# A second scaled stream for the queries, and key copies by transfer, in a two-layer decoder trunk

## The chip, the cores and the metric

One core of one Trainium2 chip runs the whole program. The metric is the time of one execution in microseconds (us) on the device; lower is better.

## What is computed

Two layers over 512 tokens of width 1024, all in float32. Layer 0 is a gated linear recurrence (HGRN2) with a gated ConvFFN behind it. Then keys and values are projected once from the normed stream. Layer 1 is differential attention with those keys and values, with a ConvFFN behind it, and a last norm. The part that matters here, cut from the reference:

```python
def rmsnorm(x, g):
    y = x32 * lax.rsqrt(jnp.mean(x32 * x32, axis=-1, keepdims=True) + EPS)
    return (y * g.astype(jnp.float32)).astype(x.dtype)

def shared_kv(x, kv_norm, kv_w):
    kv = rmsnorm(x, kv_norm) @ kv_w
    k = kv[..., :DA_QDIM].reshape(B, T, DA_HEADS, 2, DA_HEAD_DIM)
    v = kv[..., DA_QDIM:].reshape(B, T, DA_HEADS, DA_V_DIM)
...
    h = rmsnorm(x, norm_mix[li])
    q = (h @ w_q).reshape(B, T, DA_HEADS, 2, DA_HEAD_DIM) * (DA_HEAD_DIM ** -0.5)
    s = jnp.einsum('bqhcd,bkhcd->bhcqk', qb, k) + bias
    p = jax.nn.softmax(s, axis=-1)
    attn = p[:, :, 0] - lam * p[:, :, 1]
    o = jnp.einsum('bhqk,bkhv->bqhv', attn, v)
```

Keys and values read the stream scaled by `kv_norm`, queries the same stream scaled by `norm_mix[1]`; the factor of the norm, one per token, is common to both. A vector over the 1024 features can be multiplied either into the stream or into the rows of the weight.

## The kernel before

The stream lies transposed in SBUF as eight tiles `x0` to `x7` of 128 features by 512 tokens. A float32 product is made of three products of the fp32r type: each operand is split into a high part (a cast on ACT) and the rest (a subtraction on DVE), and `mm3` (lines 104 to 106) issues high by high, high by low and low by high. `split` does both halves of a split; with a gain it multiplies it in (lines 62 and 63, ACT and DVE), without one it casts and subtracts (lines 59 and 60). `x_split(n, g)` splits tile `n` into `xh`, `xl`. `on_tile`, from `stage` in `build`, is called as each tile of the new stream is done: it splits the tile, squares it on ACT and adds the square to `acc` on DVE.

Weights are streamed. `stage` (line 81) issues a load of 128 x 1024 floats on SP's queue into one of three buffers `wst`, and, if a gain is given, multiplies it in on POOL (line 86). Then `whi` is cast on ACT (line 59, or 775 in the attention) and `wlo` made on DVE (line 60, or 778), each in one of three buffers.

The attention stage, `attention`, is where the change lies. The stream reaches it unscaled (`stage("plain")`), and all 24 loads of key, query and value weights carry a gain, index 2 for keys and values and 3 for queries. The order of the work on PE, DVE, ACT and POOL is the order in which the code issues it; SP's order is left to the scheduler. There are two sequences, woven together:

- `products()` is a generator of projections, in units. A unit is one step of the sum for a key or query projection (three products of 512 columns), or two steps for a block of the values (six of 256 columns). Eight units are one projection of a head's keys, or queries, or two blocks of a pair's values. `units(n, most)` advances it by `n`, and lets `some(most)` issue up to `most` waiting steps of splitting keys and queries (`side`) and three of the small chain of a head's output norm (`chain`, lines 1047 and 160 to 166). When a projection is done, `evac` scales it by the norm's factor into `kq` (DVE, line 848); `keys` then casts each half of it into `kh` on ACT (line 869), writes a copy of the half into the other 64 partitions on POOL (line 870), and subtracts into `kl` on DVE (line 876); `queries` does likewise into `qs` (856, 859).
- The loop over `b` goes through 32 blocks of 128 queries, four a head. A block's way is: `scores` (PE, lines 980 and 981, then a masked minimum with the bias `nb` on DVE, 983), `powers` (exponentials on ACT, 989), `weigh` (the two softmaxes joined into `at`, DVE, 1004), `turn` (PE transposes `at`, 1011, ACT copies it, 1013), `gather` (PE, 1024). In one pass, `scores` is issued for block `b + 2`, `weigh` for `b + 1`, `turn` and `gather` for `b`, with 2 + 3 + 1 units of projections between them (`U1`, `U2`, `U3`).

The opening of the stage: head 0's keys and queries are projected without their last step, with the sums of `acc` (line 183) and the norm's factor (`rms`, `rows`: lines 193 to 203, the factor is `rcol_n`) between them; then come the last steps, `U0` = 8 units, and the loop. `minus_lambda` makes the scalar `lam` from a tiny product, an exponential `lme` on ACT (line 748) and two steps on DVE. `bias(h0)` fetches the bias of two heads.

Of the kernel before, what the change touches and what calls it, by code (L numbers as in the profile page):

```python
# [19 lines left out]
P = 128  # L20
T = 512
# [8 lines left out]
U0, U1, U2, U3 = 8, 2, 3, 1  # L30
PIECES = {0: 1, 1: 3, 3: 6, 6: 8}
WARM = 8

# [3 lines left out]
class Trunk:  # L37
# [34 lines left out]
        self.split(self.x[n], hi, lo, g)  # L72
        return hi, lo

    def stage(self, src, width=1024, gain=None, k0=0, cols=P):

        st = self.wp.tile([P, 1024], F32, tag="wst", name="wst", bufs=3)
        dst = st[:, :width]
        if len(src.shape) == 3:
            dst = dst.rearrange("p (n k) -> p n k", n=src.shape[1])  # L80
        self.nc.sync.dma_start(dst, src)
        if gain is not None:
            n = width // cols
            w = st[:, :width].rearrange("p (k c) -> p k c", k=n)
            g = self.gains[:, gain, k0:k0 + n].unsqueeze(2).broadcast_to([P, n, cols])
            self.nc.gpsimd.tensor_tensor(w, w, g, ALU.mult)  # L86
        return st

    def weight_tiles(self):
# [643 lines left out]
    def attention(self, xkv, acc, on_tile):  # L733
# [3 lines left out]
        with ExitStack() as ctx:  # L737
# [16 lines left out]

            nbs = {}

            def bias(h0):

                nb = nbs[h0 // 2] = ap.tile([P, 2, T], F32, tag="nb", name="nb")
                nc.gpsimd.memset(nb[:, :, 0:256], 0.0)  # L760
                rows = self.bdram[h0:h0 + 2]
                nc.sync.dma_start(nb[:, :, 256:T], bass.AP(rows.tensor, rows.offset + P - 1,
                                                           [[382, P], [P * 383, 2], [1, 256]]))


            class Load:
                def __init__(me, src, gain=None, k0=0, cols=P):
                    me.src, me.gain, me.k0, me.cols = src, gain, k0, cols

                def stage(me):  # L770
                    me.st = self.stage(me.src, 1024, me.gain, me.k0, me.cols)

                def high(me):
                    me.w = self.weight_tiles()
# [10 lines left out]
            K = [[Load(a["w_kq"][2 * h], 2)] for h in range(NH)]  # L785
            Q = [[Load(a["w_kq"][2 * h + 1], 3)] for h in range(NH)]
            V = [[Load(a["w_v"][p, hf], 2, 4 * hf, 256) for hf in range(2)] for p in range(NH // 2)]
# [56 lines left out]
            qs, ks, vs = {}, {}, {}  # L844

            def evac(ps, scale=1.0):
                t = ap.tile([P, T], F32, tag="kq", name="kq")
                v.scalar_tensor_tensor(t, ps, scale, rb, ALU.mult, ALU.mult)
                return t

# [10 lines left out]
            def keys(h, ps):  # L861

                k = evac(ps)
                hi = ap.tile([P, 2, T], F32R, tag="kh", name="kh")
                lo = kls[h % 2]
                ks[h] = hi, lo

                def high(c, own, other):
                    s.copy(hi[own, c], k[own])
                    nc.gpsimd.tensor_copy(hi[other, c], k[own])  # L870

                for c, (own, other) in enumerate(parts):
                    side.append(lambda c=c, own=own, other=other: high(c, own, other))
                for c, (own, other) in enumerate(parts):
                    side.append(lambda c=c, own=own:
                                v.tensor_tensor(lo[own, c], k[own], hi[own, c].bitcast(F32), ALU.subtract))  # L876


            def product(load, done):
                ps, (hi, lo) = self.bank(), take(load)  # L880
                for k in range(KD):
                    c = slice(k * P, (k + 1) * P)
                    self.mm3(ps, (hi[:, c], lo[:, c]), xkv[k], k == 0, k == KD - 1)
# [51 lines left out]
            def pair(p):  # L935
                yield from product(K[2 * p][0], lambda ps: keys(2 * p, ps))
                yield from product(Q[2 * p][0], lambda ps: queries(2 * p, ps))
                yield from product(K[2 * p + 1][0], lambda ps: keys(2 * p + 1, ps))
                yield from product(Q[2 * p + 1][0], lambda ps: queries(2 * p + 1, ps))
                yield from values(p, range(4))  # L940

            def products():
                yield from product(K[1][0], lambda ps: keys(1, ps))
                yield from values(0, (0, 1))
                yield from product(Q[1][0], lambda ps: queries(1, ps))
                yield from values(0, (2, 3))
                for p in range(1, NH // 2):
                    yield from pair(p)
# [19 lines left out]
            def scores(b):  # L968
                h, i = divmod(b, 4)
                if i == 0:  # L970
                    heads[h] = [self.sp.tile([P, 2, 4], F32, tag="sums", name="sums"),
                                self.sp.tile([P, 4], F32, tag="r0", name="r0"),
                                self.sp.tile([P, 4], F32, tag="oms", name="oms")]
                n = (i + 1) * P
                oi = slice(i * P, n)
                sc = [self.bank("sc")[:, :n] for c in range(2)]
                st = self.sp.tile([P, 2], F32, tag="stat", name="stat", bufs=4)
                pt = ap.tile([P, 2, T], F32, tag="p", name="p")
                for c in range(2):
                    mm(sc[c], qs[h][:, c, oi], ks[h][0][:, c, 0:n], start=True, stop=False)  # L980
                    mm(sc[c], qs[h][:, c, oi], ks[h][1][:, c, 0:n], start=False, stop=True)  # L981
                for c in range(2):
                    v.tensor_tensor_reduce(sc[c], sc[c], nbs[h // 2][:, h % 2, T - n:], 1.0, 3e38, ALU.add, ALU.min,  # L983
                                           st[:, c:c + 1])
# [44 lines left out]
            def close(h):  # L1029

                sums, r0, ms, po = heads.pop(h)
                o = ap.tile([P, T], F32, tag="o", name="o")
# [19 lines left out]
                return turn_back  # L1052

            with tc.manual_schedule(engines=ORDERED):
                first = [(self.bank("sc"), take(w[0])) for w in (K[0], Q[0])]
                steps, got = self.norm_steps(acc, "n1", "sc")
                self.proj_first(first, xkv, KD - 1, steps)
                live.clear()
                rb, rc = got[1]
                keys(0, first[0][0])  # L1060
                queries(0, first[1][0])
                some(8)
                units(2)
                split_next()
                units(2)
                split_next()
                units(U0 - 4)
# [58 lines left out]
def build(tc, a, o, stop=None):  # L1126
    nc = tc.nc
    with ExitStack() as ctx:
# [1 line left out]
        t.enter(ctx)  # L1130
        t.setup()

        def stage(g):
            acc = t.sp.tile([P, T], F32, tag="acc", name="acc")
            xs = []

            due = []

            def on_tile(n):
                for add in due:  # L1140
                    add()
                due.clear()
                if g is not None:
                    xs.append(t.x_split(n, None if g == "plain" else g))
# [123 lines left out]
```

## Time and profile before

| | us |
|---|---|
| median of 3 runs (lowest, highest) | 1261.74 (1260.07, 1262.15) |
| the profiled execution | 1260.14 |
| its span, first to last instruction | 1258.4 |
| POOL busy in the span | 76.1 |
| granted PE clock, mean | 0.995 |

The profile is one execution. Engines are PE (matrix products), PEld (its weight loads), DVE (vector), ACT (scalar), POOL (GpSimd) and SP (here only issuing transfers). A row of a timeline is start, duration, engine, line, operation, outputs, inputs, shapes and count, and in brackets the time that the engine stood idle ahead of it and what ended that. A row of groups has the busy time, the mean of one in ns, and the idle time ahead, by what ended it. The attention stage runs from about 635 to 862 us. Matmuls are pipelined: a product of 512 columns is shown as 0.39 us though the next starts 0.23 us later, so times between starts are what counts.

### The profile page before, as it was taken

The page shows a single profiled execution, that of the slowest core. Times are in us where ns is not written, and L with a number is a line of the kernel's source. Part 1 is how long each engine was busy: PE and PEld are TensorE (multiplying, and loading weights), DVE is VectorE, ACT ScalarE, POOL GpSimd, SP SyncE. Part 2 cuts the span into 40 slices and gives each one's busy share as a digit, 9 for nine tenths or more (in the row PEclk, how much of TensorE's full clock was granted, in tenths as well). Part 3 has the DMA queues.
Part 4 walks back from the last instruction along what each step waited for, and adds up shares of the span by engine and source line. Part 5 has one row for each costly group of instructions (what it writes and reads, how often), then busy time and mean ns, then how long its engine had stood idle before and what let it go on. Part 6 is the DMA issues. An engine that isn't in the chain of part 4 may idle for free.

```text
span 1258.4 us, 18026 instructions
## 1 busy us (share of the span) xinstructions
PE 1232.3 (98%) x6994; PEld 1042.5 (83%) x6994; DVE 869.6 (69%) x1651; ACT 570.4 (45%) x993; POOL 76.1 (6%) x68
## 2 busy tenths in 40 slices
PE   9999999999999999999999989999999999999997
PEld 8888898888888888888888879798888888888886
DVE  6988979587777777533467988877787777762223
ACT  6555555454444444322245556655454444442221
POOL 0000000000000000000134422200000000000001
PEclk9999999999999999999999899999999999999998
DMA  6223222133323333333232211212233333232322
GB/s 229 69 84 120 85 85 65 54 118 100 92 93 101 101 99 89 100 94 92 97 101 71 73 51 59 85 68 84 84 101 100 101 100 89 96 92 92 104 80 68
DMA packets 38269, 115.36 MB, mean 92 GB/s; under 512 B 3960, under 2 KB 9896, under 8 KB 38184
## 3 DMA queue, kind: packets, MB, share of 16 engines
q1 hardware_dynamic: 37144, 113.27, 28.4%
q8 instruction: 55, 0.90, 0.3%
q10 hardware_dynamic: 1040, 0.94, 0.2%
q14 instruction: 30, 0.25, 0.1%
HBM read 112.09 MB, written 3.68 MB: 92 GB/s over the span
## 4 chain that ended last, share of the span: by engine, by line
PE 85%; DVE 10%; ACT 3%; issue 2%; DMA 0%; POOL 0%; SPq 0%; POOLq 0%; ACTq 0%; DVEq 0%
PE mm L105 25%; PE mm L106 25%; PE mm L104 25%; DVE wlo L60 1%; DVE wlo L778 1%; PE po L1024 1%; PE sc L104 1%; PE sc L105 1%; PE sc L106 1%; PE tp L1011 1%; DVE kl L876 1%; DVE sd L473 1%; ACT whi L59 1%; DVE sc L983 1%; PE sc L981 1%
## 5 line engine op out<-in xcount | busy, mean ns | idle before, releaser
L104 PE MATMUL mm<-xh,whi 128*128 128x512 f32 x1008 | 398.4, 395 | 0.1
L105 PE MATMUL mm<-xl,whi 128*128 128x512 f32 x1008 | 394.2, 391 | 0.5 <-DVE xl L63 0.5
L106 PE MATMUL mm<-xh,wlo 128*128 128x512 f32 x1008 | 393.7, 391 | 0.0
L60 DVE TENSOR_TENSOR wlo<-wst,whi 128x1024 fp32r<-128x1024 f32 (+1 forms) x172 | 208.1, 1213 | 145.7 <-ACT whi L59 143.7
L59 ACT CAST whi<-wst 128x1024 fp32r<-128x1024 f32 (+1 forms) x172 | 177.2, 1034 | 240.9 <-PE mm L105 185.3
L106 PEld LDWEIGHTS mm<-xh,wlo 128*128 128x128 f32 x1008 | 189.7, 188 | 39.6 <-DVE wlo L778 0.2
L105 PEld LDWEIGHTS mm<-xl,whi 128*128 128x128 f32 x1008 | 190.0, 189 | 39.2 <-DVE xl L63 2.0
L104 PEld LDWEIGHTS mm<-xh,whi 128*128 128x128 f32 x1008 | 190.1, 189 | 38.8 <-ACT whi L59 0.7
L104 PE MATMUL mm<-hh,whi 128*128 128x512 f32 (+1 forms) x374 | 141.0, 377 | 0.0
L105 PE MATMUL mm<-hl,whi 128*128 128x512 f32 (+1 forms) x374 | 140.8, 377 | 0.0
L106 PE MATMUL mm<-hh,wlo 128*128 128x512 f32 (+1 forms) x374 | 140.8, 376 | 0.0
L684 DVE TENSOR_TENSOR u<-mm,rbc_f 128x512 f32<-128x512 f32 x88 | 60.2, 688 | 73.4 <-PE mm L106 73.4
L104 PEld LDWEIGHTS mm<-hh,whi 128*128 128x128 f32 x374 | 70.4, 188 | 13.0
L106 PEld LDWEIGHTS mm<-hh,wlo 128*128 128x128 f32 x374 | 70.4, 188 | 12.9
L105 PEld LDWEIGHTS mm<-hl,whi 128*128 128x128 f32 x374 | 70.4, 188 | 12.7
L86 POOL TENSOR_TENSOR wst<-wst,gains 128x1024 f32<-128x1024 f32 x24 | 49.7, 2074 | 479.1 <-DMA wst<-in_w_kq_dram 423.6
L686 ACT ACTIVATE c<-u,pack 128x512 f32<-128x512 f32 x88 | 71.5, 817 | 7.5 <-DVE u L684 3.6
L59 ACT CAST hh<-c 128x512 fp32r<-128x512 f32 x44 | 27.3, 619 | 103.0 <-DVE c L695 103.0
L104 PE MATMUL mm<-whi,xh 128*128 128x256 f32 x248 | 72.0, 290 | 0.0
L105 PE MATMUL mm<-wlo,xh 128*128 128x256 f32 x248 | 70.1, 283 | 0.6 <-DVE wlo L778 0.6
L106 PE MATMUL mm<-whi,xl 128*128 128x256 f32 x248 | 70.1, 283 | 0.0
L688 DVE SCALAR_TENSOR_TENSOR c<-u,pack,c 128x512 f32<-128x512 f32 x88 | 66.1, 751 | 2.8
(276 smaller groups left out, 1681.8 us busy)
## 6 DMA issues: line engine op xcount, KB each, us to landing
wst<-in_w_up_dram SPq DMA_DIRECT2D x88, 512.0 KB, 3.5
wst<-in_w_down_dram SPq DMA_DIRECT2D x32, 512.0 KB, 3.4
wst<-in_w_fqg_dram SPq DMA_DIRECT2D x21, 512.0 KB, 3.8
wst<-in_w_kq_dram SPq DMA_DIRECT2D x16, 512.0 KB, 3.5
wst<-in_w_down_dram SPq DMA_DIRECT2D x16, 384.0 KB, 3.0
wst<-in_w_i_dram SPq DMA_DIRECT2D x8, 512.0 KB, 3.6
wst<-in_w_ao_dram SPq DMA_DIRECT2D x8, 512.0 KB, 4.2
wst<-in_w_v_dram SPq DMA_DIRECT2D x8, 512.0 KB, 3.6
```

The source lines that it names most:

```text
L59: i = nc.scalar.copy(hi, x)
L60: j = nc.vector.tensor_tensor(lo, x, hi.bitcast(F32), ALU.subtract)
L86: self.nc.gpsimd.tensor_tensor(w, w, g, ALU.mult)
L104: mm(out, s[0], m[0], start=start, stop=False)
L105: mm(out, s[0], m[1], start=False, stop=False)
L106: mm(out, s[1], m[0], start=False, stop=stop)
L473: v.copy_predicated(dst, m, src)
L684: v.tensor_tensor(u[:, 2:], ps, rb, ALU.mult)
L686: s.activation(c, u[:, 2:], AF.Identity, bias=self.cb[:, layer, n:n + 1], scale=w(2))
L688: v.scalar_tensor_tensor(c, u[:, 0:T], w(0), c, ALU.mult, ALU.add)
L778: v.tensor_tensor(me.w[1], me.st, me.w[0].bitcast(F32), ALU.subtract)
L876: v.tensor_tensor(lo[own, c], k[own], hi[own, c].bitcast(F32), ALU.subtract))
```

## The change

The stream arrives in the attention scaled by `kv_norm` (`stage(2, True)`), and `stage` of the weights loses its gain. The queries get a stream of their own: `query_stream` splits all eight tiles once more, with gain 3, into `xqh` and `xql`; these 16 tiles fill space that `kq` and `o` (now single) and the bias (now one head at a time) give up. Keys are copied into the other half of the partitions by a transfer on SP's queue instead of by POOL.

The opening is written anew. The end of the last tile's work (its split and square) is held until the attention's first weights are asked for. Keys of heads 0 and 1 come first, then the query stream, then the queries of head 0 and two blocks of values, 16 units, ahead of the loop; `U0` is gone. In the loop, the first block of each head has one unit less.

```diff
-    def stage(self, src, width=1024, gain=None, k0=0, cols=P):
+    def stage(self, src, width=1024):
...
-        if gain is not None:
...
-            self.nc.gpsimd.tensor_tensor(w, w, g, ALU.mult)
...
-            order = [*K[0], *Q[0], *K[1], *V[0], *Q[1]]
+            order = [*K[0], *K[1], *Q[0], *V[0], *Q[1]]
...
-                t = ap.tile([P, T], F32, tag="kq", name="kq")
+                t = ap.tile([P, T], F32, tag="kq", name="kq", bufs=1)
...
-                    nc.gpsimd.tensor_copy(hi[other, c], k[own])
+                    nc.sync.dma_start(hi[other, c].bitcast(F32), hi[own, c].bitcast(F32))
...
+                def query_stream(ns):
+                    for n in ns:
+                        hi, lo = (ap.tile([P, T], F32R, tag=f"xq{part}{n}", name=f"xq{part}{n}", bufs=1)
+                                  for part in "hl")
+                        self.split(self.x[n], hi, lo, self.gain(3, n))
+                        xq.append((hi, lo))
...
+                for n in range(2):
+                    self.proj(*first[n], xkv, range(KD - 1))
+                    if n == 0:
+                        query_stream(range(2))
+                        rc = self.rms(self.sums(acc, "sc"), "n1")
+                query_stream(range(2, KD))
+                rb = self.rows(rc, "n1", "sc")
+                for n in range(2):
+                    self.proj(*first[n], xkv, [KD - 1])
                 live.clear()
...
+                for h in range(2):
+                    keys(h, first[h][0])
+                    high_next()
+                    some(2)
+                    if h == 0:
+                        some(2)
+                    low_next()
+                units(8)
+                some(2)
+                units(4)
+                split_next()
+                units(4)
                 some(8)
...
-                        if i == 0 and h % 2 == 1 and h < NH - 1:
+                        if i == 0 and h < NH - 1:
                             bias(h + 1)
...
-                    units(U2, 2)
+                    units(U2 - (b % 4 == 0), 2)
...
-        xs, acc, nxt = nxt[0], nxt[1], stage("plain")
+        xs, acc, nxt = nxt[0], nxt[1], stage(2, True)
```

Where instructions stand now. DVE in the opening, from the norm's factor (`rcol_n`) to the first projections' ends (`kq`), before:

```order
L166 SCALAR_TENSOR_TENSOR rcol_n_5994<-rs 128x4
L848 SCALAR_TENSOR_TENSOR kq<-sc,rbc_n_6019 128x512 x2
L876 TENSOR_TENSOR kl_5935<-kq,kh 64x512 x2
L859 TENSOR_TENSOR qs<-kq,qs 64x512 x2
L778 TENSOR_TENSOR wlo<-wst,whi 128x1024 x2
```

and DVE at the same place after the change (`xql` are the low parts of the query stream; lines behind 86 are five lower or so):

```order
L161 SCALAR_TENSOR_TENSOR rcol_n_5976<-rs 128x4
L63 SCALAR_TENSOR_TENSOR xql_6018<-x_74,gains,xqh_6017 128x512
L63 SCALAR_TENSOR_TENSOR xql_6022<-x_75,gains,xqh_6021 128x512
L63 SCALAR_TENSOR_TENSOR xql_6026<-x_76,gains,xqh_6025 128x512
L63 SCALAR_TENSOR_TENSOR xql_6030<-x_77,gains,xqh_6029 128x512
L63 SCALAR_TENSOR_TENSOR xql_6034<-x_78,gains,xqh_6033 128x512
L63 SCALAR_TENSOR_TENSOR xql_6038<-x_79,gains,xqh_6037 128x512
L842 SCALAR_TENSOR_TENSOR kq<-sc,rbc_n_6046 128x512
L870 TENSOR_TENSOR kl_5922<-kq,kh 64x512 x2
L772 TENSOR_TENSOR wlo<-wst,whi 128x1024
L842 SCALAR_TENSOR_TENSOR kq<-sc,rbc_n_6046 128x512
L772 TENSOR_TENSOR wlo<-wst,whi 128x1024
```

Six subtractions of the query stream stand ahead of the first `kq` (the other two stand ahead of the norm's factor), and the values' two `wlo` now come between the two heads' keys.

SP's queue in the attention, from the first bias on, before:

```order
L762 DMA nb<-bdram 128x2x256 x2
L81 DMA wst<-in_w_kq_dram 128x1024 x5
L81 DMA wst<-in_w_v_dram 128x1024 x2
L81 DMA wst<-in_w_kq_dram 128x1024
L762 DMA nb<-bdram 128x2x256
```

and SP's queue after, from the first bias to the third head's keys:

```order
L757 DMA nb<-bdram 128x256 x2
L81 DMA wst<-in_w_kq_dram 128x1024
L864 DMA kh<-kh 64x512 x2
L81 DMA wst<-in_w_kq_dram 128x1024
L864 DMA kh<-kh 64x512 x2
L81 DMA wst<-in_w_kq_dram 128x1024 x3
L81 DMA wst<-in_w_v_dram 128x1024
L757 DMA nb<-bdram 128x256
L81 DMA wst<-in_w_v_dram 128x1024
L864 DMA kh<-kh 64x512 x2
```

The 16 copies of key halves (`kh<-kh`), each waiting for ACT's cast, now stand between the weight loads.

POOL from the start of the attention, before:

```order
L86 TENSOR_TENSOR wst<-wst,gains 128x1024 x4
L760 MEMSET nb 128x2x256
L843 MEMSET kl_5935 64x512 x2
L843 MEMSET kl_5936 64x512 x2
L86 TENSOR_TENSOR wst<-wst,gains 128x1024
L870 CAST kh<-kq 64x512 x2
L86 TENSOR_TENSOR wst<-wst,gains 128x1024 x2
```

and all that POOL has in the attention after, with the first rows of the next stage:

```order
L755 MEMSET nb 128x256
L837 MEMSET kl_5922 64x512 x2
L837 MEMSET kl_5923 64x512 x2
L755 MEMSET nb 128x256 x7
L671 MEMSET u_8667 128x2
```

POOL's multiplications and casts are gone; eight memsets of the bias and four of the keys' low parts are left.

More of the change, by code (lines that the diff above doesn't have):

```diff
@@ L29 @@
 ORDERED = {mybir.EngineType.PE, mybir.EngineType.DVE, mybir.EngineType.Activation, mybir.EngineType.Pool}
-U0, U1, U2, U3 = 8, 2, 3, 1
+U1, U2, U3 = 2, 3, 1
 PIECES = {0: 1, 1: 3, 3: 6, 6: 8}
@@ L81, in stage @@
         self.nc.sync.dma_start(dst, src)
-        if gain is not None:
[L83 to L86, printed above, removed]
         return st
@@ L755, in attention, with bias, __init__ @@
             nbs = {}
[L757 to L763, printed above, removed]
+            def bias(h):
+                nb = nbs[h] = ap.tile([P, T], F32, tag="nb", name="nb")
+                nc.gpsimd.memset(nb[:, 0:256], 0.0)
+                row = self.bdram[h]
+                nc.sync.dma_start(nb[:, 256:T], bass.AP(row.tensor, row.offset + P - 1, [[382, P], [1, 256]]))
             class Load:
-                def __init__(me, src, gain=None, k0=0, cols=P):
-                    me.src, me.gain, me.k0, me.cols = src, gain, k0, cols
+                def __init__(me, src):
+                    me.src = src
                 def stage(me):
-                    me.st = self.stage(me.src, 1024, me.gain, me.k0, me.cols)
+                    me.st = self.stage(me.src)
                 def high(me):
@@ L783, in out_load @@
                 return Load(a["w_o"][2 * m:2 * m + 2, :, k0 * P:(k0 + half) * P].rearrange("n p k -> p n k"))
-            K = [[Load(a["w_kq"][2 * h], 2)] for h in range(NH)]
-            Q = [[Load(a["w_kq"][2 * h + 1], 3)] for h in range(NH)]
-            V = [[Load(a["w_v"][p, hf], 2, 4 * hf, 256) for hf in range(2)] for p in range(NH // 2)]
+            K = [[Load(a["w_kq"][2 * h])] for h in range(NH)]
+            Q = [[Load(a["w_kq"][2 * h + 1])] for h in range(NH)]
+            V = [[Load(a["w_v"][p, hf]) for hf in range(2)] for p in range(NH // 2)]
             O = [[out_load(m, k0) for m in range(KD // 2)] for k0 in (0, half)]
-            order = [*K[0], *Q[0], *K[1], *V[0], *Q[1]]
+            order = [*K[0], *K[1], *Q[0], *V[0], *Q[1]]
             for p in range(1, NH // 2):
@@ L876, in keys, with product @@
                                 v.tensor_tensor(lo[own, c], k[own], hi[own, c].bitcast(F32), ALU.subtract))
-            def product(load, done):
+            def product(load, done, xs):
                 ps, (hi, lo) = self.bank(), take(load)
@@ L933, in late_product, with key_product, query_product @@
                         yield n % 2 * half + k - half
[L935 to L940, printed above, removed]
+            def key_product(h):
+                return product(K[h][0], lambda ps: keys(h, ps), xkv)
+            def query_product(h):
+                return product(Q[h][0], lambda ps: queries(h, ps), xq)
             def products():
-                yield from product(K[1][0], lambda ps: keys(1, ps))
+                yield from query_product(0)
                 yield from values(0, (0, 1))
-                yield from product(Q[1][0], lambda ps: queries(1, ps))
+                yield from query_product(1)
                 yield from values(0, (2, 3))
                 for p in range(1, NH // 2):
-                    yield from pair(p)
+                    for h in (2 * p, 2 * p + 1):
+                        yield from key_product(h)
+                        yield from query_product(h)
+                    yield from values(p, range(4))
                 for m in range(KD // 2):
@@ L1054, in attention @@
             with tc.manual_schedule(engines=ORDERED):
-                first = [(self.bank("sc"), take(w[0])) for w in (K[0], Q[0])]
-                steps, got = self.norm_steps(acc, "n1", "sc")
-                self.proj_first(first, xkv, KD - 1, steps)
-                live.clear()
-                rb, rc = got[1]
-                keys(0, first[0][0])
-                queries(0, first[1][0])
-                some(8)
[L1063 to L1067, printed above, removed]
+                self.held()
+                first = [(self.bank("sc"), take(K[h][0])) for h in range(2)]
+                def query_stream(ns):
[13 more added lines that the diff above has]
+                    self.proj(*first[n], xkv, [KD - 1])
+                live.clear()
+                for h in range(2):
[10 more added lines that the diff above has]
+                units(4)
+                some(8)
                 for b in range(-2, 4 * NH):
@@ L1131, in build, with stage @@
         t.setup()
-        def stage(g):
+        def stage(g, hold=False):
             acc = t.sp.tile([P, T], F32, tag="acc", name="acc")
@@ L1139, in on_tile, with step @@
             def on_tile(n):
+                if hold and n == KD - 1:
+                    t.held = lambda: step(n)
+                else:
+                    step(n)
+            def step(n):
                 for add in due:
@@ L1143, in on_tile @@
                 if g is not None:
-                    xs.append(t.x_split(n, None if g == "plain" else g))
+                    xs.append(t.x_split(n, g))
                 add = t.sq_add(acc, t.x[n], n == 0, False)
```

10 lines of the change are left out of this document (5 added, 5 removed).

## The prediction

> **What bounds the kernel now.** I read the page's first part, then who waited for whom in the attention stage (635 to 862 us), then the timelines of PE, DVE and POOL around each wait found there.
>
> ```profile
> PE 1232.3 (98%) x6994; PEld 1042.5 (83%) x6994; DVE 869.6 (69%) x1651; ACT 570.4 (45%) x993; POOL 76.1 (6%) x68
> ```
>
> PE is busy all the time, so a change off PE gains only what PE waits. The rows of the waits in which PE is the one that stands (total, times, longest):
>
> ```profile
> PE tp L1011 <- DVE at L1004: 8.5, 5, 2.7
> PE po L1024 <- ACT aT L1013: 3.1, 2, 1.6
> PE mm L105 <- DVE wlo L778: 0.6, 1, 0.6
> ```
>
> That is 8.5 + 3.1 + 0.6 = 12.2 us in eight waits: PE stands at the transpose of an attention block until DVE has written `at`, or just behind it for the copy of what it transposed late, and once, in the opening, for a weight's low part. PE's timeline at the two largest waits (start, duration):
>
> ```profile
> 695.97 0.39 PE L105 MATMUL mm<-xl,whi 128*128 128x512 f32 x1
> 696.20 0.39 PE L106 MATMUL mm<-xh,wlo 128*128 128x512 f32 x1
> 699.30 0.69 PE L1011 MATMUL tp<-pack,at 128*128 128x128 f32 x2 [2.71 <-DVE at L1004]
> 700.21 0.63 PE L105 MATMUL mm<-xl,whi 128*128 128x512 f32 x1
> 703.20 0.63 PE L106 MATMUL mm<-xh,wlo 128*128 128x512 f32 x1
> 703.62 1.05 PE L1024 MATMUL po<-vt,aT 128*128 128x128 f32 x4
> 727.76 0.61 PE L1024 MATMUL po<-vt,aT 128*128 128x128 f32 x4
> 751.29 0.44 PE L1011 MATMUL tp<-pack,at 128*128 128x128 f32 x2 [2.70 <-DVE at L1004]
> ```
>
> What DVE and POOL did ahead of the first, and DVE at the same place of head 6:
>
> ```profile
> 692.53 1.75 DVE L1047 TENSOR_SCALAR ome<-oms 128x4 f32<-128x4 f32 x1
> 694.32 1.82 DVE L160 TENSOR_SCALAR rs<-ome 128x4 int32<-128x4 int32 x1
> 820.16 0.17 DVE L1047 TENSOR_SCALAR ome<-oms 128x4 f32<-128x4 f32 x1
> 820.37 0.17 DVE L160 TENSOR_SCALAR rs<-ome 128x4 int32<-128x4 int32 x1
> ```
>
> ```profile
> 689.45 2.51 POOL L870 CAST kh<-kq 64x512 fp32r<-64x512 f32 x2
> 692.04 4.08 POOL L86 TENSOR_TENSOR wst<-wst,gains 128x1024 f32<-128x1024 f32 x2
> ```
>
> Two DVE instructions on four columns take 1.75 and 1.82 us, and 0.17 us each at 820, where POOL is idle; the slow pair ends at 696.14, POOL's two multiplications at 696.12. PE's products show a second thing: they start 0.23 us apart before the wait (695.97, 696.20) and 0.43 apart behind it (eight of them from 700.21 to 703.20). The clock fell; in the stretches of the two waits (the clock is the column behind the five busy times):
>
> ```profile
> 690.00:712.00 22.00, 19.29 (x87) 15.86 (x86) 20.97 (x48) 10.97 (x29) 8.14 (x6) 0.84 0.22 68
> 745.00:762.00 17.00, 12.77 (x68) 10.25 (x67) 16.39 (x45) 9.23 (x25) 3.69 (x3) 1.00 0.15 52
> ```
>
> **What goes.** POOL loses both kinds of work that coincide with slow DVE instructions (whole run; then DVE from 648 to 858 and, the last two rows, from 812 to 870, where POOL is quiet):
>
> ```profile
> L86 POOL TENSOR_TENSOR wst<-wst,gains 128x1024 f32<-128x1024 f32 x24 | 49.7, 2074 | 479.1 <-DMA wst<-in_w_kq_dram 423.6 <-DMA wst<-in_w_v_dram 40.0 <-DVE kl L876 13.3
> L870 POOL CAST kh<-kq 64x512 fp32r<-64x512 f32 x16 | 16.9, 1054 | 20.9 <-DVE kq L848 20.0
> ```
>
> ```profile
> L778 DVE TENSOR_TENSOR wlo<-wst,whi 128x1024 fp32r<-128x1024 f32 x27 | 39.3, 1459 | 14.1 <-ACT whi L775 13.9
> L778 DVE TENSOR_TENSOR wlo<-wst,whi 128x1024 fp32r<-128x1024 f32 x8 | 9.8, 1223 | 3.8 <-ACT whi L775 3.7
> L859 DVE TENSOR_TENSOR qs<-kq,qs 64x512 fp32r<-64x512 f32 x2 | 1.4, 686 | 0.1
> ```
>
> 49.7 + 16.9 = 66.6 us leave POOL, and a `wlo` that takes 1.46 us in the mean should take 1.22. The two short instructions alone give DVE back 1.58 + 1.65 = 3.2 us ahead of the 2.71 us wait. How early DVE is with POOL idle shows at the same place of head 6:
>
> ```profile
> 823.15 0.48 DVE L1004 SCALAR_TENSOR_TENSOR at<-p,r 128x256 f32<-128x256 f32 x1
> ```
>
> ```profile
> 826.17 0.38 PE L1011 MATMUL tp<-pack,at 128*128 128x128 f32 x2
> ```
>
> `at` is done at 823.63, 2.5 us before PE asks for it. So the waits should go whole: 12.2 us. With them goes the half speed: nine products (the eight above and one ahead) at 0.43 for 0.23 us are 1.8 us, and two groups of four small matmuls behind them at 1.05 for 0.61 are 0.9: 2.7. PE also restarts late: 696.20 + 0.23 + 2.71 is 699.14, and it started at 699.30; 0.15 us at each of eight waits is 1.2. Sum of what goes: 12.2 + 2.7 + 1.2 = 16.1.
>
> The row of 690 to 712 has the half speed right behind a wait of 2.71 us, and the row of 745 to 762 has an equal wait without it; I count it to the wait, as a thing that can follow one. [...]
>
> **What is added.** In the opening ACT and DVE split the stream a second time, eight tiles each. The rows that price it (whole run), then the places where it could be felt:
>
> ```profile
> L62 ACT ACTIVATE xh<-x,gains 128x512 fp32r<-128x512 f32 x24 | 17.3, 719 | 13.4 <-DVE x L550 8.3 <-DVE x L911 3.0 <-DMA gains<-in_gains_dram 1.3
> L63 DVE SCALAR_TENSOR_TENSOR xl<-x,gains,xh 128x512 fp32r<-128x512 f32 x24 | 17.9, 747 | 7.7 <-ACT xh L62 7.6
> ```
>
> ```profile
> 638.77 0.17 ACT L748 ACTIVATE lme<-mm 128x2 f32<-128x2 f32 x1
> 641.72 0.16 DVE L193 TENSOR_SCALAR rms_n<-sc 128x4 f32<-128x4 f32 x1 [0.89 <-PE sc L183]
> 643.69 0.16 DVE L166 SCALAR_TENSOR_TENSOR rcol_n<-rs 128x4 f32<-128x4 f32 x1
> 646.40 0.60 PE L188 MATMUL sc<-pack,rcol_n 128*128 128x128 f32 x4
> 647.80 1.31 DVE L848 SCALAR_TENSOR_TENSOR kq<-sc,rbc_n 128x512 f32<-128x512 f32 x2 [3.95 <-PE sc L106]
> 648.23 0.39 PE L104 MATMUL mm<-xh,whi 128*128 128x512 f32 x1
> 687.84 1.26 ACT L869 CAST kh<-kq 64x512 fp32r<-64x512 f32 x2
> 706.05 0.23 PE L980 MATMUL sc<-kh,qs 128*128 128x128 f32 x1
> ```
>
> Five of ACT's eight stand ahead of `lme`: 5 x 0.72 = 3.6, so `lme` ends near 642.5, and DVE's `rms_n`, queued behind `lam`, starts near 642.9, not 641.72. The factor, 2.1 us behind it, is ready at 645.0; PE asks at 646.40: nothing. Six of DVE's eight follow: 6 x 0.75 = 4.5, to 649.5, so the first `kq` is 1.7 us later than 647.80. PE now has 16 units ahead of the first scores (a unit is three products, or six of half the width, 0.7 us) and reaches them at 648.2 + 16 x 0.7 = 659.4. Until then DVE has three `kq`, four `kl` and two `qs`, all at 0.69 by the rows, and two `wlo`: 9 x 0.69 + 2 x 1.22 = 8.7, to 658.2. Covered, by 1.2 us. Tighter is the second `wlo` of the values: 649.5 + 4 x 0.69 (two `kq`, two `kl`) + 2 x 1.22 = 654.7; PE wants it 10 units in, at 655.2. I book 0.5 us, between 0 and 1.5 for a DVE that starts an instruction or two late.
>
> The copies of the keys become transfers on SP. No row shows a copy inside the chip. I bound one by POOL's 1.05 us below and the bias's transfer above, and take 3, nearer to the transfer:
>
> ```profile
> nb<-bdram SPq DMA_DIRECT2D x4, 256.0 KB, 3.9
> ```
>
> ```profile
> 676.33 0.33 SPq L81 DMA_DIRECT2D wst<-in_w_kq_dram  x1
> 686.90 1.05 ACT L775 CAST whi<-wst 128x1024 fp32r<-128x1024 f32 x1
> ```
>
> For head 0 the cast ends at 649.5 + 0.69 + 1.26 = 651.5, so the copy lands by 655.4, against scores at 659.4. For head 2 the cast ended at 689.1 and the scores came at 706.05. Both ends of the bound cost nothing. On SP each copy waits for ACT's cast, with weight loads queued behind it: counting loads and casts in order, the load of 676.33 is the one cast at 686.90, 10.6 us later, and others wait longer, so a hold of one block (four to six units and its small matmuls, under 6 us) costs nothing.
>
> The bias per head, its smaller memsets, and the scaled split at the end of the first FFN (ACT's 0.72 us, once in some 15 us) lie under PE's products: nothing. Each head's first block gives one unit, 0.7 us, to the opening: of the 2.5 us shown at 823.63 it leaves 1.8. Since products fall at other places of DVE's queue now, I book 0.6 for small new waits, between 0 and B's 4.8 below.
>
> Sum: 16.1 - 0.5 - 0.6 = 15.0. The profiled execution took 1260.14 us (1258.4 of it the span): 1245.1. The runs' median, 1261.74, is 1.6 above it. A clock that halves behind a wait in one run and not in the next would spread runs so; with the waits gone I carry 0.7 of the 1.6 over: **1245.8 us**.
>
> **The rivals.** A, the forecast: 0.70, from 1242.5 to 1248.
>
> B: DVE stays late in some heads. One unit of cover less, and a `wlo`, a `kq` and two `kl` (1.22 + 3 x 0.69 = 3.3 us) now often between two scores. For it: they are more than the slack of 1.8. Against: DVE can give back in the next block. If six heads wait 0.8 each, 4.8 return: 1250.6. Chance 0.16.
>
> C: the half speed has another cause than the wait and stays: 1245.8 + 2.7 = 1248.5. For it: the equal wait at 751.29 without it. Against: it begins with PE's first product behind the wait. Chance 0.05. [...]
>
> D: the change doesn't do what it says, since DVE is slowed by weights landing and not by POOL. For it: loads land shortly before POOL works on them. Against: the slow pair ends with POOL's. The waits stay, the opening costs 0.5: 1262.2. Chance 0.04.
>
> E, slower: the copies come late. Place: the first scores of a head. It decides once a copy lands over 17 us (689.1 to 706.05) after its cast, that is, when SP holds it for three blocks behind loads that wait for buffers. Then, at 2 us a head and with the clock falling once more, 8 x 2 + 2.7 = 18.7 come for the 16.1 that go: 1261.74 + 18.7 + 1.1 - 16.1 = 1265.4. Against: loads are issued 10 us and more before they are used. Chance 0.05.
>
> **How the numbers follow.** Faster by over 0.2% (2.5 us, about what a measurement of this kernel tells from no change) are A, B and C: 0.91; within 0.2% is D: 0.04; slower is E: 0.05. The range takes A's low end (all 16.1 goes and 1.6 of spread, with nothing added, would be 1244 by the profiled run; a further 1.5 for waits that no row names) and reaches past B: 1242.5 to 1253.
>
> **What would show it.** Right: POOL has only memsets from 610 to 860; `wlo` is at 1.22 and `kl` and `qs` at 0.69 in the mean; PE waits less than 0.5 us for any `at`; the clock is 1.00 in every stretch; the attention is some 15 us shorter. Wrong: PE stands at the scores for a transfer (E), `at` is late with the short instructions at 0.17 (B), or they still take 1.8 with POOL idle (D).

## The result, and the profile after

The changed kernel takes 1249.03 us, the median of 4 runs (1247.66 to 1250.46). The kernel before takes 1260.9 (4 runs, 1259.95 to 1262.15). The ratio is 0.9904, with a 95% interval of 0.9892 to 0.9917. That is 11.9 us faster, where 15.9 (1261.74 to 1245.8) were forecast. The time lies inside the range of 1242.5 to 1253, but 3.2 us above the predicted one. The profiled execution took 1250.46. Lines of the changed kernel have numbers 4 to 6 lower than before: `at` is line 1000, `wlo` 772, `kl` 870, `yl` 1040.

The first part of the page after, then from the list of waits PE's only one in the attention over half a microsecond (total, times, longest):

```profile
PE 1230.5 (99%) x6994; PEld 1042.3 (83%) x6994; DVE 842.9 (68%) x1659; ACT 576.0 (46%) x1001; POOL 10.1 (1%) x32
```

```profile
PE tp L1007 <- DVE yl L1040: 3.5, 3, 2.0
```

POOL has 10.1 us for 76.1, DVE 842.9 for 869.6. PE's waits for `at` and `aT`, 11.6 us, are gone. A wait that was not there before has come, of 3.5 us for `yl`. DVE's groups in the attention after (mean in ns behind the bar), to be held against 1459 for `wlo`:

```profile
L772 DVE TENSOR_TENSOR wlo<-wst,whi 128x1024 fp32r<-128x1024 f32 x28 | 34.2, 1221 | 12.6 <-ACT whi L769 12.5
L853 DVE TENSOR_TENSOR qs<-kq,qs 64x512 fp32r<-64x512 f32 x16 | 11.0, 687 | 3.7 <-ACT qs L850 3.4
L870 DVE TENSOR_TENSOR kl<-kq,kh 64x512 fp32r<-64x512 f32 x16 | 11.0, 685 | 4.2 <-ACT kh L863 4.0
```

All are at the durations that the prediction gave them for an idle POOL, 1.22 and 0.69 us. To measure the stage alone, I take the time from the tiny product for `lam`, with which it begins, to the first product of the second FFN. PE's timeline of before, and then of after:

```profile
635.43 0.38 PE L746 MATMUL mm<-lmp,ones 64*128 64x2 f32 x2
883.58 0.39 PE L104 MATMUL mm<-xh,whi 128*128 128x512 f32 x1
```

```profile
637.37 0.38 PE L741 MATMUL mm<-lmp,ones 64*128 64x2 f32 x2
874.17 0.39 PE L99 MATMUL mm<-xh,whi 128*128 128x512 f32 x1
```

The stage went from 248.15 to 236.80 us: 11.35 gained. The prediction had the attention some 15 us shorter. That the stage starts 1.9 us later is not the change's doing: a second profiled execution of the same kernel (below, `changed_again`) starts it at 635.15.

Where the new wait stands: PE's timeline after, in head 6, then DVE's and ACT's just ahead of it.

```profile
793.97 0.60 PE L1037 MATMUL tp<-pack,o 128*128 128x128 f32 x4
799.07 0.55 PE L1007 MATMUL tp<-pack,at 128*128 128x128 f32 x3 [1.96 <-DVE yl L1040]
799.37 0.60 PE L99 MATMUL mm<-xqh,whi 128*128 128x512 f32 x1
802.75 0.51 PE L101 MATMUL mm<-xqh,wlo 128*128 128x512 f32 x1
803.10 0.83 PE L1020 MATMUL po<-vt,aT 128*128 128x128 f32 x6
```

```profile
794.65 0.62 DVE L1000 SCALAR_TENSOR_TENSOR at<-p,r 128x384 f32<-128x384 f32 x1
795.19 0.68 DVE L842 SCALAR_TENSOR_TENSOR kq<-mm,rbc_n 128x512 f32<-128x512 f32 x1
796.56 1.41 DVE L870 TENSOR_TENSOR kl<-kq,kh 64x512 fp32r<-64x512 f32 x2 [0.69 <-ACT kh L863]
798.26 0.75 DVE L1040 SCALAR_TENSOR_TENSOR yl<-tp,subg,yh 128x512 fp32r<-128x512 f32 x1 [0.30 <-ACT yh L1039]
```

```profile
795.91 1.26 ACT L863 CAST kh<-kq 64x512 fp32r<-64x512 f32 x2 [0.67 <-DVE kq L842]
797.19 0.37 ACT L1023 ACTIVATE sq<-po,r 128x128 f32<-128x128 f32 x1
797.55 0.68 ACT L1039 ACTIVATE yh<-tp,subg 128x512 fp32r<-128x512 f32 x1
```

`at` is ready at 795.3; PE comes to it at 797.1 and stands until 799.07. What PE lacks is the bank `tp`, the piece of PSUM that transposes are written to. There is one such bank (`tp=(1, 1)` where `attention` asks for its banks); the finished head before was transposed back into it at 793.97, and it comes free only when ACT (`yh`) and DVE (`yl`) have read it. Both stand behind the next head's keys: ACT's two casts `kh`, DVE's `kq` and two `kl`. Behind the wait the nine products from 799.37 to 803.10 take 3.73 us where nine at 0.23 take 2.07: 1.7 more, at half speed. The same wait is 0.29 us in head 2 and 1.23 in head 4.

### The profile page after: what moved, and what is told of

Its sections match the earlier page's. It is cut to its first block, busy times and chain, and to the rows that moved or that the text cites. A ratio compares the mean times of both kernels' runs of the same rounds, so it can differ in the third digit from the quotient of the medians.

```text
span 1248.6 us, 17998 instructions
## 1 busy us (share of the span) xinstructions
PE 1230.5 (99%) x6994; PEld 1042.3 (83%) x6994; DVE 842.9 (68%) x1659; ACT 576.0 (46%) x1001; POOL 10.1 (1%) x32
## 4 chain that ended last, share of the span: by engine, by line
PE 62%; issue 30%; DVE 5%; ACT 2%; DMA 1%; POOL 0%; SPq 0%; POOLq 0%; ACTq 0%; DVEq 0%
PE mm L101 18%; PE mm L99 18%; PE mm L100 17%; PE po L1020 1%; DVE wlo L60 1%; PE tp L1007 1%; PE sc L99 1%; PE sc L100 1%; PE sc L101 1%; PE sc L977 1%; PE sc L976 1%; PE at L490 1%; DVE wlo L772 0%; DMA raw<-in_w_fqg_dram 0%; DVE sc L979 0%
## 5 line engine op out<-in xcount | busy, mean ns | idle before, releaser
L99 PE MATMUL mm<-xh,whi 128*128 128x512 f32 x944 | 371.3, 394 | 0.8 <-ACT whi L59 0.7
L100 PE MATMUL mm<-xl,whi 128*128 128x512 f32 x944 | 368.7, 391 | 0.6 <-DVE xl L63 0.5
L101 PE MATMUL mm<-xh,wlo 128*128 128x512 f32 x944 | 368.1, 390 | 0.0
L100 PEld LDWEIGHTS mm<-xl,whi 128*128 128x128 f32 x944 | 177.6, 188 | 37.6 <-DVE xl L63 2.1
L99 PEld LDWEIGHTS mm<-xh,whi 128*128 128x128 f32 x944 | 177.6, 188 | 37.4 <-ACT whi L59 1.3
L101 PEld LDWEIGHTS mm<-xh,wlo 128*128 128x128 f32 x944 | 177.4, 188 | 37.0 <-DVE wlo L60 0.2
L683 DVE SCALAR_TENSOR_TENSOR c<-u,pack,c 128x512 f32<-128x512 f32 x88 | 66.1, 751 | 2.7
L682 DVE SCALAR_TENSOR_TENSOR c<-u,pack,c 128x512 f32<-128x512 f32 x88 | 65.4, 745 | 0.0
```

The costliest lines, as they stand in the source:

```text
L99: mm(out, s[0], m[0], start=start, stop=False)
L100: mm(out, s[0], m[1], start=False, stop=False)
L101: mm(out, s[1], m[0], start=False, stop=stop)
L682: v.scalar_tensor_tensor(c, u[:, 1:T + 1], w(1), c, ALU.mult, ALU.add)
L683: v.scalar_tensor_tensor(c, u[:, 0:T], w(0), c, ALU.mult, ALU.add)
```

## The experiments

First theory: POOL's multiplications, which read and write weights in SBUF, hold up DVE while they run; without them all of the old waits go, and what is missing of the forecast is the wait for `yl`, made by the units of products that the change moved out of the loop. Rivals stand in the expectations. The table has all runs; "stage" is measured as above, from two rows of PE's timeline of the run's one profiled execution, and the waits are PE's in it, from 0.5 us up.

| run | median us | ratio to before (95%) | stage us | waits of PE, us |
|---|---|---|---|---|
| changed_again | 1248.43 | 0.9905 (0.9891 to 0.9919) | 236.85 | `yl` 3.5 |
| before_no_gains | 1244.39 | 0.9873 (0.9859 to 0.9887) | 231.17 | none |
| before_copies_sent | 1256.29 | 0.9966 (0.9954 to 0.9979) | 242.75 | `at` 5.3, `aT` 3.1 |
| pool_multiplies | 1262.36 | 1.001 (1.0001 to 1.0019) | 249.99 | `yl` 7.8, `aT` 2.2, `at` 1.0, `kq` 0.5 |
| pool_reads | 1257.92 | 0.9964 (0.995 to 0.9979) | 244.84 | `yl` 6.6, `aT` 1.0, `kq` 0.5 |
| pool_writes | 1249.44 | 0.9904 (0.989 to 0.9917) | 236.95 | `yl` 3.6 |
| before_unit_moved | 1250.41 | 0.992 (0.9905 to 0.9934) | 237.07 | `yl` 3.9 |
| early_back | 1247.74 | 0.9891 (0.9876 to 0.9906) | 234.70 | `yl` 2.8 |
| back_then_casts | 1243.95 | 0.9872 (0.9857 to 0.9888) | 231.88 | none |
| pool_casts_keys | 1248.71 | 0.991 (0.9893 to 0.9926) | 236.80 | `yl` 4.0, `kq` 0.7 |
| one_stream | 1249.23 | 0.9911 (0.9896 to 0.9926) | 236.66 | `yl` 3.5 |

**The changed kernel once more**, unaltered.

> The changed kernel itself, as a yardstick on the same chip: 1249 within 1.5.

1248.43, and the stage is the same within 0.05 us.

**One part of POOL's work at a time, in the kernel before.**

```diff
-                    me.st = self.stage(me.src, 1024, me.gain, me.k0, me.cols)
+                    me.st = self.stage(me.src)
```

> The kernel before, with POOL's multiplications of the staged weights left out (the gains of the norms are thus left out of queries, keys and values); POOL still casts the copies of the keys. If the multiplications are what slows DVE: `wlo` at 1.22 to 1.26 us, the two short instructions ahead of the wait at 696 at 0.17 each, PE's waits in the attention down from 12.2 to 2 to 5 us, and 1247 to 1252. If the casts do it: waits of 8 to 11 and 1257 to 1260.

1244.39, under the range of 1247 to 1252: every wait went, more than I expected, though POOL still casts the keys.

```diff
-                    nc.gpsimd.tensor_copy(hi[other, c], k[own])
+                    nc.sync.dma_start(hi[other, c].bitcast(F32), hi[own, c].bitcast(F32))
```

> The kernel before, with the copies of the keys as transfers on SP, and POOL still multiplying. If the multiplications are what slows DVE: `wlo` stays near 1.45 us, `kl` falls from 1.07 to some 0.8, and 1257 to 1260. If the casts do it: 1247 to 1252. If transfers of keys come late at the scores: PE waits there for `kh`, and the time is above 1261.

1256.29, a little under the expected 1257. `wlo` stays at 1.46 us; `kl` falls to 0.79. So the multiplications cost 15.9 us by the medians (1260.29 in these runs to 1244.39), and the casts 4.0 as long as the multiplications are there. The two don't add up to 19.9: `back_then_casts` (below), which has neither, is 16.3 under 1260.29. That a wait ends only with the last of its causes would explain this; no run shows it by itself.

**POOL's work put back into the changed kernel.** Three kinds, after each load of a key, query or value weight (cut from the code; `junk` is a scratch tile of 256 columns). The first is the multiplication of before, by ones; the second only reads the weight; the third reads one column, so as to start in time, and then only writes:

```diff
+ w = me.st.rearrange("p (k c) -> p k c", k=me.n)
+ nc.gpsimd.tensor_tensor(w, w, self.ones[:, 0:me.n].unsqueeze(2).broadcast_to([P, me.n, 1024 // me.n]), ALU.mult)
```

> The changed kernel, in which POOL multiplies each staged weight of queries, keys and values by ones, in the place where the kernel before multiplied by the gains (same instruction, same size, 24 loads; the products are unchanged). First theory: POOL's multiplications slow DVE. Then `wlo` goes from 1.22 back to about 1.4 us in the mean, four-column instructions next to POOL's show 1.6 to 1.8 us again, PE waits some 8 to 12 us for `at`, and the time is 1256 to 1264. Rival: weights that land slow DVE, not POOL; then DVE's means stay and the time is that of the changed kernel, 1249 within 2. Second rival: POOL costs because ACT has to wait for it before it can cast a weight; then DVE's means stay at 1.22 and 0.69, and PE waits for `whi` and `wlo`.

```diff
+ for j in range(4):
+     w = me.st[:, j * 256:(j + 1) * 256].rearrange("p (k c) -> p k c", k=2)
+     nc.gpsimd.tensor_tensor(junk.rearrange("p (k c) -> p k c", k=2), w,
+                             self.ones[:, 0:2].unsqueeze(2).broadcast_to([P, 2, P]), ALU.mult)
```

> The changed kernel, in which POOL reads each staged weight of queries, keys and values in four multiplications of 256 columns and writes a small scratch tile that nobody reads; no engine waits for POOL's result. First theory (POOL's reading slows DVE): about as with the multiplication in place, DVE's `wlo` near 1.4 us and 1254 to 1264 us. Rival (POOL costs by the chain load, POOL, ACT): 1249 within 2, with `wlo` at 1.22.

```diff
+ nc.gpsimd.tensor_copy(junk[:, 0:1], me.st[:, 0:1])
+ for j in range(6):
+     nc.gpsimd.memset(junk, 0.0)
```

> The changed kernel, in which POOL, for each staged weight of queries, keys and values, copies one column of it and then only writes: six memsets of 256 columns on a scratch tile that nobody reads, about as long as the multiplication. If any work of POOL slows DVE: `wlo` near 1.4 us and 1254 to 1264 us, as with reading. If only POOL's instructions that read do: `wlo` at 1.22 to 1.25 and 1249 within 2.

The multiplications take back the whole gain and a little more: 13.3 us over the changed kernel's 1249.03. Reads that nobody waits for take 8.9. Writes take 0.4, within the noise, though POOL is as long at work: 53.6 us, where the multiplications took 48.3 and the reads 74.8. POOL's groups of the run that writes:

```profile
L770 POOL MEMSET junk<- 128x256 f32 x144 | 45.1, 313 | 8.3
L768 POOL COPY junk<-wst 128x1 f32<-128x1 f32 x24 | 8.5, 356 | 479.4 <-DMA wst<-in_w_kq_dram 438.4 <-DMA wst<-in_w_v_dram 41.0
```

The expectation missed two things: PE's waits are for `yl` more than for `at`, and from 648 to 862 us `wlo` is at 1.22 us with the multiplications and at 1.24 with the reads, not at 1.4. In this order of work other instructions meet POOL; with the multiplications:

```profile
L874 DVE TENSOR_TENSOR kl<-kq,kh 64x512 fp32r<-64x512 f32 x16 | 16.6, 1038 | 3.9 <-ACT kh L867 3.6
L857 DVE TENSOR_TENSOR qs<-kq,qs 64x512 fp32r<-64x512 f32 x16 | 13.6, 849 | 3.1 <-ACT qs L854 2.7
L1002 DVE SCALAR_TENSOR_TENSOR r<-sums,r,lam 128x1 f32<-128x1 f32 x32 | 12.4, 389 | 0.0
```

`kl` has 1.04 us for 0.69, and PE's wait for `yl`, which stands behind `kl`, grows from 3.5 to 7.8. The longest of these waits, from the timelines of POOL, DVE and PE:

```profile
757.49 2.48 POOL L768 TENSOR_TENSOR wst<-wst,ones 128x1024 f32<-128x1024 f32 x1 [7.73 <-DMA wst<-in_w_kq_dram]
758.13 3.10 DVE L874 TENSOR_TENSOR kl<-kq,kh 64x512 fp32r<-64x512 f32 x2
761.27 0.75 DVE L1044 SCALAR_TENSOR_TENSOR yl<-tp,subg,yh 128x512 fp32r<-128x512 f32 x1
762.08 0.90 PE L1011 MATMUL tp<-pack,at 128*128 128x128 f32 x3 [4.69 <-DVE yl L1044]
```

The two `kl` take 3.10 us for 1.41, and `yl`, which ends at 762.02, ends the wait. The rival of landing weights falls: they land in all of these runs. The chain load, POOL, ACT is no large part either: PE's waits there for a weight part are 0.3 us in sum. How one DVE instruction is held up, from the timelines of DVE and of POOL in the run with the multiplications:

```profile
747.69 0.16 DVE L160 TENSOR_TENSOR rs<-rs 128x4 f32<-128x4 f32 x1
747.89 1.89 DVE L161 SCALAR_TENSOR_TENSOR rs<-rs 128x4 f32<-128x4 f32 x1
749.81 0.16 DVE L159 SCALAR_TENSOR_TENSOR rs<-rs,ome 128x4 f32<-128x4 f32 x1
```

```profile
747.86 1.90 POOL L768 TENSOR_TENSOR wst<-wst,ones 128x1024 f32<-128x1024 f32 x1 [5.91 <-DVE rs L160]
```

POOL's instruction starts 0.03 us ahead of DVE's, and both end together, at 749.76 and 749.78.

**The units that were moved**, without the rest of the change, in the kernel before without the gains. Eight more units stand ahead of the loop, and the first block of each of the eight heads has one less:

```diff
+                split_next()
+                units(8)
                 for b in range(-2, 4 * NH):
...
-                    units(U2, 2)
+                    units(U2 - (b % 4 == 0), 2)
```

> The kernel before without POOL's multiplications (the gains are left out, as in the run without them, 1244.4 us and no wait for `yl`), with the opening and the first blocks as the change has them: 16 units of products ahead of the first scores in place of 8, and one unit less in the first block of each head. Nothing else of the change is in it. First theory: that unit moves the end of the key product, so that `kh` and `kl` come ahead of `yh` and `yl` in heads 2, 4 and 6, and this is the wait that the changed kernel has left: PE waits 3 to 4 us for `yl` in three places, some product behind the longest runs at half speed, and the time is 1248 to 1250.5. Rival: the wait comes of the transfers or of the queries' second stream; then no wait for `yl`, and 1243.5 to 1245.5.

1250.41, inside the range of 1248 to 1250.5, and the wait for `yl` is there in the same three heads, 0.27, 1.62 and 2.01 us. DVE at the place of head 6 without the move (`before_no_gains`):

```profile
790.06 1.22 DVE L778 TENSOR_TENSOR wlo<-wst,whi 128x1024 fp32r<-128x1024 f32 x1
791.20 0.74 DVE L1044 SCALAR_TENSOR_TENSOR yl<-tp,subg,yh 128x512 fp32r<-128x512 f32 x1
791.86 0.68 DVE L848 SCALAR_TENSOR_TENSOR kq<-mm,rbc_n 128x512 f32<-128x512 f32 x1
...
794.42 1.40 DVE L876 TENSOR_TENSOR kl<-kq,kh 64x512 fp32r<-64x512 f32 x2
```

There `yl` comes ahead of `kq` and `kl`. The move alone costs 5.9 us of the stage (231.17 to 237.07), all that the changed kernel lacks. The units put back in the changed kernel were not tried; two other ways of giving `yl` its place were.

**`yl` earlier.** First the place of `back()`, which issues the transposition back with `yh` and `yl`, one unit earlier; then, shown against this first edit, the keys' steps held back until `yh` and `yl` are issued (`units(n, 0)` issues no such step, `units(1, 4)` up to four):

```diff
-                    units(U2 - (b % 4 == 0), 2)
+                    if b % 4 == 1 and b > 1:
+                        units(U2 - 1, 2)
+                        back()
+                        units(1, 2)
+                    else:
+                        units(U2 - (b % 4 == 0), 2)
                     gather(b)
                     low_next()
-                    if b % 4 == 1 and b > 1:
-                        back()
```

> The changed kernel, with the transposition back of a finished head issued one unit of products earlier. First theory: the three waits left in the attention (3.5 us) are for the one `tp` bank, which `yl` frees late because `kl` and `wlo` stand ahead of it on DVE; issued earlier, `yl` comes ahead of a part of them. Then PE waits less than 0.5 us for `yl`, no stretch of the attention has a clock under 1.00, and 3.5 + three late restarts of 0.15 + 1.7 of half speed go: about 1243.4 us against the changed kernel's 1249.0 (1242.5 to 1245.5). Rival: DVE is short of time in these blocks whatever it does first; then the same 3 us come back as waits for `at` or at the scores, and the time stays within 1.5 us of 1249. Second rival: the half speed has a cause of its own; then the waits go and the clock stays at 0.90 in some stretch, about 1245.

1247.74, above the theory's range. By the number alone it fits the first rival (within 1.5 us of 1249), but not by its mechanism: no wait for `at` or at the scores came. Head 2 waits no more; heads 4 and 6 still wait 1.20 and 1.59 us, for ACT's `yh` stood behind the two casts `kh` as before. The clock is 1.00 in every stretch of the attention.

```diff
-                        units(U2 - 1, 2)
+                        units(U2 - 1, 0)
                         back()
-                        units(1, 2)
+                        units(1, 4)
```

> The changed kernel, with the transposition back of a finished head one unit earlier, as in the run before, and with the casts and subtractions of the next head's keys and queries held back for the two units ahead of it, so that ACT's `yh` and DVE's `yl` stand ahead of `kh` and `kl` in their queues. In the run with the earlier place alone ACT's two casts `kh` still stood ahead of `yh` in heads 4 and 6, and 2.8 us of waits for `yl` stayed. Theory: it is the order in the queues; then the waits for `yl` go (under 0.3 us) and the time is 1244 to 1246.5, at least 1.5 us under the earlier place alone (1247.7). Rival: DVE and ACT lack time there; then `kh` and `kl` are late instead, PE waits as long at the scores or at the next `wlo` or `at`, and the time is 1247 to 1250.

1243.95, just under the range that the theory gave (1244 to 1246.5), and below both kernels: 0.9872 of before (0.9857 to 0.9888), and 4.5 us under the changed kernel on the same chip. DVE and PE in head 6:

```profile
792.55 0.68 DVE L842 SCALAR_TENSOR_TENSOR kq<-mm,rbc_n 128x512 f32<-128x512 f32 x1
793.21 0.75 DVE L1040 SCALAR_TENSOR_TENSOR yl<-tp,subg,yh 128x512 fp32r<-128x512 f32 x1
793.92 1.41 DVE L870 TENSOR_TENSOR kl<-kq,kh 64x512 fp32r<-64x512 f32 x2
```

```profile
794.33 0.49 PE L1007 MATMUL tp<-pack,at 128*128 128x128 f32 x3
```

PE waits for nothing there, and `kl` is late for nobody: the same instructions in another order. DVE and ACT don't lack time; the rival falls.

**The copies and the second stream**, each undone alone in the changed kernel: the copies on POOL again, and `xq.append(xkv[n])` in place of the second split.

> The changed kernel, with the copies of the keys cast by POOL again, as before the change, in place of the transfers. First theory: with the multiplications gone POOL's casts meet little of DVE's work (`kl` at 0.70 us in the kernel before without the gains); 1248 to 1250. Rival: the casts slow `kl` ahead of `yl`, and the three waits grow by 0.3 us each or more: 1250 to 1253. Second rival: the transfers cost time: under 1247.

> The changed kernel without the queries' second stream: the queries read the keys' stream, and ACT's and DVE's eight instructions each in the opening are gone (the queries' gains are thus left out). The prediction booked 0.5 us for them, between 0 and 1.5; the profile after shows 0.3 of a wait and 0.5 of a pause of PE there. First theory: 1247.6 to 1248.6 against 1248.4. Rival: the split holds up the start of the attention more than its waits show: under 1247.

1248.71 and 1249.23, against 1248.43: neither can be told from no change (the second is above its range of 1247.6 to 1248.6, by less than its own runs spread), and the stage is within 0.2 us of 236.85 in both. `kl` is at 0.83 us with POOL's casts, and the waits for `yl` are 0.5 longer, but the clock is 1.00 in every stretch of that execution's attention, which would make up for it.

## Why the prediction was right, and where it was off

**What goes: 16.1 booked.** Right, and 0.9 low. In the kernel before without the multiplications 17.0 us of the stage went (248.15 to 231.17). All 12.2 us of waits went, and no stretch of the attention had a clock under 1.00. The half speed went with the waits, as booked. The cause was narrower than I had it: I set both kinds of POOL's work against DVE, and once the multiplications are gone the casts cost nothing that shows.

**The opening: 0.5 booked.** Right, within its 0 to 1.5. Without the second split the stage is shorter by no more than 0.2 us in one execution. The steps, in the timeline after:

```profile
643.83 0.17 ACT L743 ACTIVATE lme<-mm 128x2 f32<-128x2 f32 x1
650.31 0.68 DVE L842 SCALAR_TENSOR_TENSOR kq<-sc,rbc_n 128x512 f32<-128x512 f32 x1
661.32 0.22 PE L976 MATMUL sc<-kh,qs 128*128 128x128 f32 x1
```

With the 1.9 us of later start, I had `lme` done near 644.4, the first `kq` at 651.4 and the scores at 661.3. `kq` came 1.1 us early, the scores to the tenth.

**The copies of the keys: nothing booked, a landing of 3 us taken.** Right; the view of the tile `kh` has this for its 16 transfers:

```profile
DMA to landing us min/median/max: 2.2/2.2/3.9
```

PE never stood for one, so E is out; but the transfers brought nothing either.

**New small waits: 0.6 booked, between 0 and 4.8.** This is the step that failed. The changed kernel's stage is 5.6 us over the 231.17 without multiplications. Up to 0.2 of it is the opening; the rest is 3.5 of waits, 1.7 of half speed, and 0.2 to 0.4 left over, in which late restarts may lie. So 17.0 went where 16.1 was booked, and 5.6 came where 0.5 + 0.6 was: the stage gained 11.4 us, not 15.0. I had measured the slack of `at` in head 6, 2.5 us, taken one moved unit's 0.7 from it, and relied on the rest. For `at` that held: PE waited for none. But the move also shifted the end of the key product, and with it `kh`, `kq` and `kl`, in front of `yh` and `yl`. I had not followed who waits for those two: the next transposition, for the only bank `tp`. So it is B that happened in kind (DVE late in some heads behind `kq` and two `kl`), though not for `at`, and in three heads rather than six. The time, 1249.0, is outside A's 1242.5 to 1248 and nearer to B's 1250.6 than to the forecast. The range held because it reached past B, for a wait that the prediction did not name: that much is luck.

**The clock.** C had the half speed come of something else than a wait. With all waits gone in `back_then_casts` and `before_no_gains`, no stretch of the attention is under 1.00, so it comes with waits. But not with every one: behind some 2 us at the place of head 6 it came in six executions (1.96 three times, 1.97 twice, 2.01) and not in a seventh (2.06, `pool_casts_keys`). I had expected 1.00 everywhere; the stretch of that wait after says 0.90:

```profile
795.00:812.00 17.00, 15.04 (x96) 13.44 (x95) 11.41 (x32) 10.17 (x27) 0.00 (x0) 0.90 0.26 77
```

**The spread: 0.7 carried over.** No run shows this term by itself. With the waits for `yl` left, the changed kernel's four runs spread over 2.8 us, but over 0.3 in `changed_again`; the four without a wait (`before_no_gains`) spread over 1.5.

**D** is out by the runs that put POOL's work back.

## What to carry to other kernels

POOL's time is not free because POOL has time to spare: here its instructions that read weights held up DVE, and through DVE's queue PE. 48.3 us of multiplications cost 13.3 us, 74.8 us of reads 8.9, and 53.6 us of work that writes, but for one column a weight, 0.4. Before units of work are shifted in a hand-written order, list what comes ahead of each reader of a buffer that exists once; the slack of the value that the next step reads says nothing about the bank that it is written to. Issue what frees a single buffer before the next item's preparation.

## What the runs showed of the hardware

In `pool_multiplies` DVE was held for the whole of one of POOL's multiplications: 1.89 us at 747.89 for an instruction of four columns that takes 0.16 in the median. In `pool_reads`, with POOL's work in pieces of 256 columns, the longest such instruction took 0.58. In `pool_writes` 45.1 us of POOL's memsets left DVE's `wlo` at 1.22 and `kl` and `qs` at 0.69. `ome`, which has one input, was held as well before the change: 1.75 us at 692.53, beside POOL's two multiplications, for 0.17 at 820.16.

In the attention stages of these runs PE has 14 waits over 1.9 us (1.96 to 4.69), and behind 12 of them, or still in them, the clock fell to 0.50; behind 2.06 (`pool_casts_keys`) and 2.70 (before, at 751.29) it did not, nor behind any of some 1.8 or less. By the mean clock of the stretches it stood at 0.50 for some 3.5 us ten times (after, from 799.6 to 803.0) and for some 7 us twice (before, from 698.5, still in the wait that ends at 699.30, to 705.4, and `pool_reads` behind 3.51 us).
